# A gated-delta-rule mixer on one Trainium2 core: diagonal blocks of 43 rows instead of 32, two applications of W instead of three, and the decay matrices of a group of heads made one product earlier

## The chip, the cores and the metric

The kernel runs on one core of a Trainium2 chip. The time is the device time of one execution in microseconds (us): 2797.3 us, the median of three runs (2796.41 to 2797.56). The profile is of one execution of its own. The names of the engines are those of the profile: PE is the matrix engine (its weight loads are listed apart as PEld), DVE the vector engine, ACT the scalar engine, POOL GpSimd; SP is the queue that issues most of the DMAs.

## The reference

A two-layer decoder trunk on 256 tokens of width 2048. Each layer is a mixer, a layer norm, a gated feed-forward network, a layer norm and a gated addition. The change touches only the first layer's mixer, a gated delta rule with 16 query/key heads and 32 value heads of 128:

```python
qkv = silu(causal_dwconv(x @ w_in ..., conv_w)); q, k = l2norm(q) * 128 ** -0.5, l2norm(k)
beta = sigmoid(b); g = -exp(a_log) * softplus(a + dt_bias); gc = cumsum(g)
lmat = where(strict, (kb @ k.T) * decay, 0)          # decay = exp(gc_i - gc_j)
sol = triangular_solve(lmat + eye, [vb, kb * exp(gc)])
... o = q_dec @ S + (q k decay) @ v_new;  o * rsqrt(mean(o^2)) * norm_g * silu(z);  o @ w_o
```

The heart is a unit lower triangular system (I + L) u = rhs for each value head and each chunk of tokens.

## The kernel before, in words

**Products.** Every product with a weight matrix reads the weights in tiles of 512 KB (`weights`, L99 to L121): the SP queue fetches `raw` (four buffers), ACT makes a rounded copy `hi` (L114), DVE the rest `lo` (L115; three buffers of each), and PE multiplies with both. A tile of a transposed product (`gemm_t_steps`) is 8 matmuls of 512 columns (L147) and 8 of 256 columns (L151); one `next` or `yield` is one tile. The products of the gate z (`gemm_steps`) are L184, L187 and L190.

**Groups.** The mixer works in chunks of 128 tokens (two chunks, `a` = 0 and 1) and in eight groups g of four value heads, so a group has eight triangular systems of 128 rows (q = 8 in the shapes). The loop at the end of `gdn_groups` does for each g, in program order: `values(g)` (8 tiles of weights), `keys(g + 1)` (4 tiles for k, then 4 for q), `zgate(g + 1)` (8 tiles), `inverses(g)`, `front(g + 1)`, `mixes(g + 1)`, `substitute(g + 1)`, `solve(g)`, `outputs(g)`. For g = 0 `front`, `substitute` and `zgate` of group 0 lie inside or behind `values(0)`; for g = 7 the place of the next group's products is taken by `ahead`, twelve steps of the output product.

**One group's solution.** `front` makes L: `decays` fetches a row of sums `qd` and makes the decays on ACT (L494, L495), `sums` multiplies k with itself on PE (`g_ps<-k`, L542, L543) and makes small vectors on DVE, `blocks` makes L on DVE (L574) and sends its diagonal blocks through DRAM, so that one partition holds one block: four writes `lt` (L579) and four reads `ld` (L583), all on SP. `causal` prepares the masks for the outputs and n21, which couples the two chunks. `substitute` inverts the diagonal blocks of 32 rows on POOL, row by row: 31 steps of one multiplication (L612) and one subtraction (L614) in the tile `xi`, spread over partitions by block, head and a quarter of the columns. The result goes through DRAM: four writes `tt` (L617), four reads `pm` (L631, in `inverses`), all issued by POOL. Then `inverses` multiplies L by the block inverses (`w_ps<-pm,L`, L623) and copies what lies off the diagonal blocks to W. `solve` applies the block inverse to the right side (`s_ps<-vt,pm`) and then W three times (`s_ps<-y,W`), each followed by a subtraction on DVE (L691); with four blocks W is nilpotent of order four, and three applications are exact. It does so for chunk 0, couples by n21 (`s_ps<-u,n`), and does the same for chunk 1. In the trace, an fp32 matmul of one head has two records, so a product of four heads has eight.

**What sets the order.** The instructions are written in program order, and a planner orders each engine's instructions ahead of time by that priority and its own costs: where one isn't ready by its reckoning, a later one goes first. The splits `hi` and `lo` have a raised priority, and so has `front` of group 0. On the chip each engine runs its list in that fixed order. A tile with one buffer (L, pm, W, `ld`) can be written again only when its last reader is done.

Of the kernel before, what the change touches and what calls it, by code (L numbers as in the profile page):

```python
# [30 lines left out]
C_IDENT, C_TRI, C_QMIN, C_CMIN, C_CAUSAL, C_XINIT, C_ONES = 0, 128, 256, 384, 512, 640, 896  # L31
N_CONST = 1024


def constants():
# [6 lines left out]
    x = np.zeros((4, 32, 8, 32), np.float32)  # L42
    for cg in range(4):
        for k in range(8):
            x[cg, :, k, 4 * k + cg] = 1.0
    c[:, C_XINIT:C_XINIT + 256] = x.reshape(P, 256)
    c[:, C_ONES:C_ONES + P] = 1.0
# [16 lines left out]
class Trunk:  # L64
    def __init__(self, nc, tc, ctx, t):
# [16 lines left out]
        cst = self.cst = self.cp.tile([P, N_CONST - P], F32, tag="cst", name="cst")  # L82
        self.tri = cst[:, C_TRI - P:C_TRI - P + P]
        self.cmin = cst[:, C_CMIN - P:C_CMIN - P + P]
        self.xinit = cst[:, C_XINIT - P:C_XINIT - P + 256]
        self.ones = cst[:, C_ONES - P:C_ONES - P + P]
# [278 lines left out]
    def gdn_gates(self, pool, w, gk):  # L365
# [42 lines left out]
        nc.tensor.matmul(pc[:, 64:96], self.ones, g[:, 0], start=True, stop=True)  # L408
# [8 lines left out]
    def gdn(self, ahead):  # L417
# [3 lines left out]
        with tc.tile_pool(name="gk", bufs=1) as gk, tc.tile_pool(name="gw", bufs=1) as pool:  # L421
# [6 lines left out]
            w = pool.tile([P, 1024], F32, tag="L", name="gates")  # L428
            def load(nb, to=None):
# [3 lines left out]
                for a in range(2):  # L433
# [4 lines left out]
                         1: [(cr, t["gdn_conv_w"].rearrange("k (n c) -> n k c", c=P)), (self.cst, t["cst"][:, P:]),  # L438
# [14 lines left out]
    def gdn_groups(self, pool, gk, cw, ng, oT, load, taps, gates, ahead):  # L453
# [31 lines left out]
        def decays(s):  # L485
# [5 lines left out]
            L = s["L"] = pool.tile([P, 2, 4, P], F32, tag="L", name="L")  # L491
# [4 lines left out]

        def causal(s):

            g, dm = s["g"], s["qd"]
            do = s["qo"] = pool.tile([P, 4, P], F32, tag="qo", name="qo", bufs=2)  # L500
            for h in h4:
                nc.scalar.activation(do[:, h], dm[:, 1, h], AF.Exp, bias=self.gout[:, 4 * g + h:4 * g + h + 1])
            n21 = s["n21"] = pool.tile([P, 4, P], F32, tag="n21", name="n21", bufs=2)
            nc.vector.tensor_tensor(five(n21), bcast(s["gram"][0][:, :, P:S], 2, 2), five(do), op=ALU.mult)
# [63 lines left out]
        def blocks(s):  # L568
# [8 lines left out]
            lt = self.dr.tile([8, 4, 32, 32], F32, tag="lt", name="lt")  # L577
            for b in range(4):
                nc.sync.dma_start(out=lt[:, b].rearrange("q i j -> i q j"),  # L579
                                    in_=L[32 * b:32 * b + 32, :, :, 32 * b:32 * b + 32].rearrange("p a h j -> p (a h) j"))  # L580
            ld = s["ld"] = pool.tile([P, 32, 32], F32, tag="ld", name="ld")
            for e in h4:
                nc.sync.dma_start(out=ld[32 * e:32 * e + 32], in_=bass.AP(tensor=lt.tensor, offset=lt.offset,  # L583
                                                                          ap=[[1024, 32], [1, 1024]]))

        def mixes(s):
# [8 lines left out]
            for h in range(2):  # L595
                for a in range(2):
                    nc.tensor.matmul(pss[:, 2 * h + a:][:, 0:1], s["sq"][:, h, a * P:(a + 1) * P],
                                     self.ones[:, 0:1], start=True, stop=True)
# [4 lines left out]
        def substitute(s):  # L603


            ld = s["ld"]
            xi = pool.tile([P, 8, 32], F32, tag="xi", name="xi", bufs=2)
            tmp = pool.tile([P, 8, 32], F32, tag="xt", name="xt", bufs=2)
            nc.gpsimd.tensor_copy(xi, self.xinit.rearrange("p (c j) -> p c j", c=8))
            for i in range(31):  # L610
                w, m = 31 - i, i // 4 + 1
                nc.gpsimd.tensor_tensor(tmp[:, :m, :w], bcast(ld[:, i + 1:, i], m, 1),  # L612
                                        xi[:, :m, i:i + 1].to_broadcast([P, m, w]), op=ALU.mult)
                nc.gpsimd.tensor_tensor(xi[:, :m, i + 1:], xi[:, :m, i + 1:], tmp[:, :m, :w], op=ALU.subtract)  # L614
            tt = s["tt"] = self.dr.tile([8, 4, 8, 4, 32], F32, tag="tt", name="tt")
            for e in range(4):
                nc.gpsimd.dma_start(out=tt[:, :, :, e].rearrange("q b c j -> (q b) c j"), in_=xi[32 * e:32 * e + 32])  # L617
# [572 lines left out]
```

## Time and profile before

| what | before |
|---|---|
| median of three runs | 2797.3 us |
| the profiled execution's own time | 2797.12 us |
| its span, first to last instruction | 2795.1 us |
| PE busy | 2776.6 us (99%) |
| weight loads on PE | 2390.1 us (86%) |
| DVE busy | 1856.2 us (66%) |
| ACT busy | 1421.6 us (51%) |
| POOL busy | 337.7 us (12%) |
| DMA | 520.82 MB, mean 186 GB/s |

The span starts with the first instruction. The first mixer takes about the first 756 us of it; from group 1 to group 6 its groups repeat every 85.4 us. In a row of a timeline the first number is the start and the second the time to the end of the last of a merged row's instructions; a number behind "x" counts instructions. Matmuls overlap, so the price of a row on PE is the distance from its start to the start of the row behind it.

### The profile page before, as it was taken

How to read it: one execution, taken by the hardware profiler on the slowest of the kernel's cores; microseconds unless marked ns; L12 is line 12 of the kernel's file. 1: busy time of each engine (PE TensorE's matmuls, PEld its weight loads, DVE VectorE, ACT ScalarE, POOL GpSimd, SP SyncE). 2: the span in 40 equal slices, each digit the busy share in tenths (PEclk: the TensorE clock that was granted, in tenths of full speed). 3: DMA queues.
4: the chain of work that ended last, by engine and by line, in shares of the span. 5: the costliest groups of instructions: out<-in, count | busy, mean ns of one | idle time of the engine just before them, and what ended most of it. 6: DMA issues, size and time to landing. Idle time of an engine off the chain costs nothing. (4 is left out here: it accounts for less than half of the span.)

```text
span 2795.1 us, 40216 instructions
## 1 busy us (share of the span) xinstructions
PE 2776.6 (99%) x14958; PEld 2390.1 (86%) x14958; DVE 1856.2 (66%) x3059; ACT 1421.6 (51%) x2239; POOL 337.7 (12%) x688
## 2 busy tenths in 40 slices
PE   8999999999999999999999999999999999999999
PEld 7888888888888888888888889888888888888887
DVE  6787787877556666666545665776676666655566
ACT  4555566555445555555434544455465555543453
POOL 1543234442200000000000000120000000000000
PEclk9999999999999999999999999999999999999999
DMA  7755665655565666666556567655556666665655
GB/s 213 205 157 158 166 176 164 168 152 159 173 210 164 193 206 206 207 196 207 196 191 208 171 198 215 181 152 163 181 181 196 197 187 199 194 195 195 207 171 195
DMA packets 412275, 520.82 MB, mean 186 GB/s; under 512 B 28940, under 2 KB 301712, under 8 KB 411824
## 3 DMA queue, kind: packets, MB, share of 16 engines
q1 hardware_dynamic: 404912, 499.91, 58.9%
q0 software_dynamic: 7168, 18.35, 2.7%
q8 instruction: 117, 1.92, 0.3%
q14 instruction: 78, 0.64, 0.1%
HBM read 513.94 MB, written 7.39 MB: 187 GB/s over the span
## 5 line engine op out<-in xcount | busy, mean ns | idle before, releaser
L115 DVE TENSOR_TENSOR lo<-raw,hi 128x1024 fp32r<-128x1024 f32 (+1 forms) x921 | 1125.0, 1223 | 606.0 <-ACT hi L114 594.6
L114 ACT ACTIVATE hi<-raw 128x1024 fp32r<-128x1024 f32 (+1 forms) x921 | 967.9, 1053 | 698.9 <-PE b_ps L187 469.5
L147 PE MATMUL mm_ps<-xT,hi 128*128 128x512 f32 (+1 forms) x4176 | 1027.9, 394 | 2.6 <-ACT hi L114 2.3
L147 PEld LDWEIGHTS mm_ps<-xT,hi 128*128 128x128 f32 (+1 forms) x4176 | 762.0, 188 | 148.9 <-ACT hi L114 2.9
L151 PEld LDWEIGHTS mm_ps<-xT,lo 128*128 128x128 f32 (+1 forms) x4176 | 539.4, 191 | 22.7 <-DVE lo L115 1.5
L151 PE MATMUL mm_ps<-xT,lo 128*128 128x256 f32 (+1 forms) x4176 | 557.2, 284 | 0.4 <-DVE lo L115 0.4
L184 PE MATMUL b_ps<-hi,xT 128*128 128x512 f32 (+1 forms) x704 | 270.9, 386 | 0.0
L187 PE MATMUL b_ps<-hi,xT 128*128 128x512 f32 (+1 forms) x704 | 268.8, 383 | 0.0
L220 ACT ACTIVATE fold<-mm_ps 128x256 f32<-128x256 f32 x261 | 98.1, 376 | 268.1 <-PE mm_ps L147 267.8
L184 PE MATMUL b_ps<-hi,hTA 128*128 128x512 f32 x512 | 199.3, 389 | 0.0
L187 PE MATMUL b_ps<-hi,hTA 128*128 128x512 f32 x512 | 199.2, 389 | 0.0
L190 PE MATMUL b_ps<-lo,xT 128*128 128x512 f32 (+1 forms) x704 | 188.4, 383 | 0.0
L239 POOL DMA_DIRECT2D lng<-in_ln_g x16 | 8.8, 547 | 1239.1 <-PE b_ps L190 654.5
L612 POOL TENSOR_TENSOR xt<-ld,xi 128x60 f32<-128x60 f32 (+24 forms) x248 | 116.2, 468 | 345.1 <-DMA ld<-lt 326.3
L187 PEld LDWEIGHTS b_ps<-hi,xT 128*128 128x128 f32 x704 | 132.2, 188 | 24.8
L184 PEld LDWEIGHTS b_ps<-hi,xT 128*128 128x128 f32 x704 | 132.2, 188 | 24.1
L190 PEld LDWEIGHTS b_ps<-lo,xT 128*128 128x128 f32 x704 | 129.9, 188 | 24.5
L190 PE MATMUL b_ps<-lo,hTA 128*128 128x512 f32 x512 | 136.8, 389 | 0.0
L190 PEld LDWEIGHTS b_ps<-lo,hTA 128*128 128x128 f32 x512 | 96.1, 188 | 20.0
L184 PEld LDWEIGHTS b_ps<-hi,hTA 128*128 128x128 f32 x512 | 96.1, 188 | 20.0
L187 PEld LDWEIGHTS b_ps<-hi,hTA 128*128 128x128 f32 x512 | 96.1, 188 | 19.9
L614 POOL TENSOR_TENSOR xi<-xi,xt 128x60 f32<-128x60 f32 (+24 forms) x248 | 107.5, 433 | 19.4
(266 smaller groups left out, 2571.0 us busy)
## 6 DMA issues: line engine op xcount, KB each, us to landing
raw<-in_gdn_w_in SPq DMA_DIRECT2D x193, 512.0 KB, 4.4
raw<-in_ffn_w_gate SPq DMA_DIRECT2D x160, 512.0 KB, 4.4
raw<-in_ffn_w_up SPq DMA_DIRECT2D x160, 512.0 KB, 4.6
raw<-in_ffn_w_down SPq DMA_DIRECT2D x160, 512.0 KB, 4.1
raw<-in_dsa_w_in SPq DMA_DIRECT2D x72, 512.0 KB, 3.7
raw<-in_gdn_w_o SPq DMA_DIRECT2D x64, 512.0 KB, 4.0
raw<-in_ple_w_gate SPq DMA_DIRECT2D x64, 512.0 KB, 4.9
raw<-in_dsa_w_o SPq DMA_DIRECT2D x32, 512.0 KB, 3.9
```

The lines of the kernel that those rows point to most:

```text
L114: act = nc.scalar.activation(hi, raw, AF.Copy)
L115: ins = nc.vector.tensor_tensor(lo, raw, hi.bitcast(F32), op=ALU.subtract)
L147: ins = nc.tensor.matmul(q[:m, :], hi[:, k, o:o + m], x[:, k0 + k].rearrange("p a b -> p (a b)"), start=k0 + k == 0, stop=last)
L151: ins = nc.tensor.matmul(q[:m, S:], lo[:, k, o:o + m], x[:, k0 + k, 0, :], start=False, stop=last)
L184: ins = nc.tensor.matmul(ps[a][:, :n], xh, hi, start=k == 0, stop=False)
L187: self.before = nc.tensor.matmul(ps[a][:, :n], xl, hi, start=False, stop=False)
L190: self.last = nc.tensor.matmul(ps[a][:, :n], x(k)[:, 0, a * P:(a + 1) * P], lo, start=False, stop=k == kt - 1)
L220: nc.scalar.activation(t[:m], ps[:, S:], AF.Copy)
L239: ins = self.nc.gpsimd.dma_start(out=r, in_=bass.AP(tensor=src.tensor, offset=src.offset, ap=[[0, P], [1, n]]))
L612: nc.gpsimd.tensor_tensor(tmp[:, :m, :w], bcast(ld[:, i + 1:, i], m, 1), xi[:, :m, i:i + 1].to_broadcast([P, m, w]), op=ALU.mult)
L614: nc.gpsimd.tensor_tensor(xi[:, :m, i + 1:], xi[:, :m, i + 1:], tmp[:, :m, :w], op=ALU.subtract)
```

## The change

The diagonal blocks become 43 rows high, from rows 0, 43 and 85 (the second and the third share row 85). With three blocks W is nilpotent of order three, and W is applied twice. POOL's substitution gets 42 steps in place of 31, on 96 partitions in place of 128, with up to 132 elements a step. A block's left 22 columns and its right 21 go to DRAM and back as two tiles, `ld` and `ldr`, in six writes of 48 or 32 rows and eight reads; the inverses come back in six reads of 32 and 16 rows in place of four. The start value of `xi` is fetched from DRAM by POOL's queue for each group instead of being copied from a constant in SBUF, and the tiles `xi`, `xt` and `qo` have one buffer each in place of two. The constant of ones goes; its users take a tile set for that, or the last column of `tri`.

L gets two buffers. In the loop `front(g + 1)` moves from behind `inverses(g)` to before `zgate(g + 1)` (for g = 0, to behind `zgate(1)`, followed by seven of the eight tiles of group 1's value product). `causal` and `mixes` leave that place for `values` of their own group; n21 is made by a new function `cross` that stays in `front`, for which ACT makes the same four exponentials once more.

```diff
-C_IDENT, C_TRI, C_QMIN, C_CMIN, C_CAUSAL, C_XINIT, C_ONES = 0, 128, 256, 384, 512, 640, 896
-N_CONST = 1024
+C_IDENT, C_TRI, C_QMIN, C_CMIN, C_CAUSAL, C_XINIT = 0, 128, 256, 384, 512, 640
+B_ROWS, B_COLS, B_LEFT = 43, 11, 22
+B_FROM = (0, 43, 85)
+N_CONST = C_XINIT + B_COLS * B_ROWS
...
-            L = s["L"] = pool.tile([P, 2, 4, P], F32, tag="L", name="L")
+            L = s["L"] = pool.tile([P, 2, 4, P], F32, tag="L", name="L", bufs=2)
...
+        def cross(s):
+
+            n21 = s["n21"] = pool.tile([P, 4, P], F32, tag="n21", name="n21", bufs=2)
+            for h in h4:
+                nc.scalar.activation(n21[:, h], s["qd"][:, 1, h], AF.Exp, bias=self.gout[:, 4 * s["g"] + h:4 * s["g"] + h + 1])
+            nc.vector.tensor_tensor(five(n21), bcast(s["gram"][0][:, :, P:S], 2, 2), five(n21), op=ALU.mult)
+
         def causal(s):
 
             g, dm = s["g"], s["qd"]
-            do = s["qo"] = pool.tile([P, 4, P], F32, tag="qo", name="qo", bufs=2)
+            do = s["qo"] = pool.tile([P, 4, P], F32, tag="qo", name="qo")
...
-            n21 = s["n21"] = pool.tile([P, 4, P], F32, tag="n21", name="n21", bufs=2)
-            nc.vector.tensor_tensor(five(n21), bcast(s["gram"][0][:, :, P:S], 2, 2), five(do), op=ALU.mult)
...
-            lt = self.dr.tile([8, 4, 32, 32], F32, tag="lt", name="lt")
-            for b in range(4):
-                nc.sync.dma_start(out=lt[:, b].rearrange("q i j -> i q j"),
-                                    in_=L[32 * b:32 * b + 32, :, :, 32 * b:32 * b + 32].rearrange("p a h j -> p (a h) j"))
-            ld = s["ld"] = pool.tile([P, 32, 32], F32, tag="ld", name="ld")
-            for e in h4:
-                nc.sync.dma_start(out=ld[32 * e:32 * e + 32], in_=bass.AP(tensor=lt.tensor, offset=lt.offset,
-                                                                          ap=[[1024, 32], [1, 1024]]))
+            nl = B_ROWS - B_LEFT
+            parts = []
+            for k, n, o, tall, tag in ((B_ROWS, B_LEFT, 0, 48, "ld"), (nl, nl, B_LEFT, 32, "ldr")):
+                lead = B_FROM[-1] + o + tall - P
+                lt = self.dr.tile([8, 3, lead + tall, n], F32, tag="lt" + tag, name="lt")
+                for b, r in enumerate(B_FROM):
+                    c = r + o
+                    r0 = min(c, P - tall)
+                    at = lead - c + r0
+                    nc.sync.dma_start(out=lt[:, b, at:at + tall].rearrange("q i j -> i q j"),
+                                      in_=L[r0:r0 + tall, :, :, c:c + n].rearrange("p a h j -> p (a h) j"))
+                ld = pool.tile([96, k, n], F32, tag=tag, name="ld")
+                parts.append((lt, ld, k * n, (lead + tall) * n, lead * n))
+            for lt, ld, m, step, at in parts:
+                for e in h4:
+                    nc.sync.dma_start(out=ld[24 * e:24 * e + 24], in_=bass.AP(tensor=lt.tensor, offset=lt.offset + at,
+                                                                              ap=[[step, 24], [1, m]]))
+            s["ld"] = [x[1] for x in parts]
...
-            ld = s["ld"]
-            xi = pool.tile([P, 8, 32], F32, tag="xi", name="xi", bufs=2)
-            tmp = pool.tile([P, 8, 32], F32, tag="xt", name="xt", bufs=2)
-            nc.gpsimd.tensor_copy(xi, self.xinit.rearrange("p (c j) -> p c j", c=8))
-            for i in range(31):
-                w, m = 31 - i, i // 4 + 1
-                nc.gpsimd.tensor_tensor(tmp[:, :m, :w], bcast(ld[:, i + 1:, i], m, 1),
-                                        xi[:, :m, i:i + 1].to_broadcast([P, m, w]), op=ALU.mult)
-                nc.gpsimd.tensor_tensor(xi[:, :m, i + 1:], xi[:, :m, i + 1:], tmp[:, :m, :w], op=ALU.subtract)
+            ld, right = s["ld"]
+            xi = pool.tile([96, B_COLS, B_ROWS], F32, tag="xi", name="xi")
+            nc.gpsimd.dma_start(out=xi, in_=t["cst"][:96, C_XINIT:])
+            for i in range(B_ROWS - 1):
+                w, m = B_ROWS - 1 - i, i // 4 + 1
+                col = ld[:, i + 1:, i] if i < B_LEFT else right[:, i + 1 - B_LEFT:, i - B_LEFT]
+                tmp = pool.tile([96, 132], F32, tag="xt", name="xt")[:, :m * w].rearrange("p (c j) -> p c j", c=m)
+                nc.gpsimd.tensor_tensor(tmp, bcast(col, m, 1), xi[:, :m, i:i + 1].to_broadcast([96, m, w]), op=ALU.mult)
+                nc.gpsimd.tensor_tensor(xi[:, :m, i + 1:], xi[:, :m, i + 1:], tmp, op=ALU.subtract)
...
-            for b in range(4):
-                nc.gpsimd.dma_start(out=pm[32 * b:32 * b + 32, :, 32 * b:32 * b + 32],
-                                    in_=s["tt"][:, b].rearrange("q c e j -> (c e) q j"))
+            for b, r in enumerate(B_FROM):
+                o = int(b > 1)
+                for k, n in ((o, 32), (B_ROWS - 16, 16)):
+                    nc.gpsimd.dma_start(out=pm[r + k:r + k + n, :, r + o:r + B_ROWS],
+                                        in_=s["tt"][:, b].rearrange("q c e j -> (c e) q j")[k:k + n, :, o:])
...
-                mul(s["L"][:, a], pm[:, 4 * a:4 * a + 4, 32:], ps)
+                mul(s["L"][:, a], pm[:, 4 * a:4 * a + 4, B_ROWS:], ps)
...
+            else:
+                causal(s)
+                if g > 1:
+                    for _ in range(3):
+                        next(steps)
+                mixes(s)
             self.go_(steps)
...
-                for i in range(3):
+                for i in range(2):
                     ps = mul(W[:, a], y)
...
-            causal(s)
+            cross(s)
...
                 n = keys(g + 1, rest)
+                if g:
+                    front(n)
                 zgate(n, [])
+                if not g:
+                    front(n)
+                    for _, _ in zip(range(7), begin(n)[0]):
+                        pass
...
             inverses(s)
             if g < 7:
-                front(n)
-                mixes(n)
                 substitute(n)
             solve(s)
```

`begin` makes the steps of a group's value product once and hands them to `values` again.

More of the change, by code (lines that the diff above doesn't have):

```diff
@@ L41, in constants @@
     c[:, C_CMIN:C_CMIN + P] = np.where(j <= i, np.float32(3.4e38), np.float32(-BIG))
[L42 to L47, printed above, removed]
+    x = np.zeros((4, 24, B_COLS, B_ROWS), np.float32)
+    for n in range(B_ROWS):
+        x[n % 4, :, n // 4, n] = 1.0
+    c[:96, C_XINIT:] = x.reshape(96, B_COLS * B_ROWS)
     c[:, C_CAUSAL:C_CAUSAL + P] = j <= i
@@ L407, in gdn_gates @@
         nc.tensor.matmul(pc[:, 0:64], self.tri, g64, start=True, stop=True)
-        nc.tensor.matmul(pc[:, 64:96], self.ones, g[:, 0], start=True, stop=True)
+        ones = pool.tile([P, P], F32, tag="y0", name="ones")
+        nc.gpsimd.memset(ones, 1.0)
+        nc.tensor.matmul(pc[:, 64:96], ones, g[:, 0], start=True, stop=True)
         nc.tensor.matmul(pc[:64, 128:256], g64, self.tri, start=True, stop=True)
@@ L427, in gdn @@
             cr = pool.tile([64, 4, P], F32, tag="ld", name="cr")
-            w = pool.tile([P, 1024], F32, tag="L", name="gates")
+            w = pool.tile([P, 1024], F32, tag="L", name="gates", bufs=2)
             def load(nb, to=None):
@@ L628, in inverses, with begin @@
         def inverses(s):
-            for b in range(4):
-                nc.gpsimd.dma_start(out=pm[32 * b:32 * b + 32, :, 32 * b:32 * b + 32],
-                                    in_=s["tt"][:, b].rearrange("q c e j -> (c e) q j"))
-            for a in range(2):
-                ps = self.sp.tile([P, 4, 96], F32, tag="bk", name="w_ps")
-                mul(s["L"][:, a], pm[:, 4 * a:4 * a + 4, 32:], ps)
-                for b in (1, 2, 3):
-                    nc.scalar.activation(W[:32 * b, a, :, 32 * b:32 * b + 32], ps[:32 * b, :, 32 * b - 32:32 * b], AF.Copy)
+            for b, r in enumerate(B_FROM):
[3 more added lines that the diff above has]
+                                        in_=s["tt"][:, b].rearrange("q c e j -> (c e) q j")[k:k + n, :, o:])
+            for a in range(2):
+                ps = self.sp.tile([P, 4, P - B_ROWS], F32, tag="bk", name="w_ps")
+                mul(s["L"][:, a], pm[:, 4 * a:4 * a + 4, B_ROWS:], ps)
+                for r, n in ((B_ROWS, B_ROWS), (2 * B_ROWS, P - 2 * B_ROWS)):
+                    nc.scalar.activation(W[:r, a, :, r:r + n], ps[:r, :, r - B_ROWS:r - B_ROWS + n], AF.Copy)
+        def begin(s):
+            g = s["g"]
+            v = pool.tile([P, 4, S], F32, tag="v", name="v")
+            if "v" in s:
+                return s["v"]
+            s["v"] = self.gemm_t_steps(w_in, 4096 + 512 * g, 512, self.xT, conv(32 + 4 * g, lambda n: v[:, n])), v
+            return s["v"]
         def values(s):
             g = s["g"]
-            v = pool.tile([P, 4, S], F32, tag="v", name="v")
-            steps = self.gemm_t_steps(w_in, 4096 + 512 * g, 512, self.xT, conv(32 + 4 * g, lambda n: v[:, n]))
+            steps, v = begin(s)
             if not g:
```

15 lines of the change are left out of this document (7 added, 8 removed).

## The prediction, made before the changed kernel was run

> **What bounds the kernel now.** I read the page first, its busy times and slices.
>
> ```profile
> span 2795.1 us, 40216 instructions
> PE 2776.6 (99%) x14958; PEld 2390.1 (86%) x14958; DVE 1856.2 (66%) x3059; ACT 1421.6 (51%) x2239; POOL 337.7 (12%) x688
> POOL 1543234442200000000000000120000000000000
> PEclk9999999999999999999999999999999999999999
> ```
>
> PE has work for 99% of the span at the full granted clock, and POOL's substitution fills only the first eleven slices. Second, the waits of PE up to 1000 us:
>
> ```profile
> PE t_ps L231 <- DMA x_in<-in_x: 5.1, 1, 5.1
> PE mm_ps L147 <- ACT hi L114: 2.3, 2, 1.8
> ```
>
> The first is the start of the kernel. In the groups PE waits for nothing worth naming: neither for the weights, nor for POOL's chain, nor for DVE between two applications of W, since the planner puts weight matmuls between them. So a matmul taken away is time taken away, as long as no new wait appears. Third, PE's timeline, for the price of what goes and the place of what moves:
>
> ```profile
> 138.80 1.92 PE L623 MATMUL w_ps<-pm,L 128*128 128x96 f32 x16
> ...
> 202.27 0.48 PE L184 MATMUL b_ps<-hi,xT 128*128 128x512 f32 x1
> ...
> 204.20 1.07 PE L190 MATMUL b_ps<-lo,xT 128*128 128x512 f32 x4
> ...
> 206.92 1.07 PE L190 MATMUL b_ps<-lo,xT 128*128 128x512 f32 x4
> ...
> 224.16 1.92 PE L623 MATMUL w_ps<-pm,L 128*128 128x96 f32 x16
> 225.91 0.62 PE L542 MATMUL g_ps<-k 128*128 128x256 f32 x2
> ...
> 227.25 1.06 PE L623 MATMUL s_ps<-vt,pm 128*128 128x128 f32 x8
> 228.06 2.10 PE L147 MATMUL mm_ps<-xT,hi 128*128 128x512 f32 x8
> 230.00 2.07 PE L151 MATMUL mm_ps<-xT,lo 128*128 128x256 f32 x16
> 231.91 3.82 PE L147 MATMUL mm_ps<-xT,hi 128*128 128x512 f32 x16
> 235.56 2.08 PE L151 MATMUL mm_ps<-xT,lo 128*128 128x256 f32 x16
> ...
> 243.52 1.05 PE L623 MATMUL s_ps<-y,W 128*128 128x128 f32 x8
> 244.33 1.19 PE L151 MATMUL mm_ps<-xT,lo 128*128 128x256 f32 x8
> 245.36 1.15 PE L623 MATMUL s_ps<-y,W 128*128 128x128 f32 x8
> 246.27 1.20 PE L151 MATMUL mm_ps<-xT,lo 128*128 128x256 f32 x8
> ```
>
> The product for W (`w_ps`) comes every 224.16 - 138.80 = 85.4 us. Before the second one stand the z products, from 202.27 on (21.9 us); behind it stand the products k with k (1.34 us, to 227.25), which begin the next group's L. A tile of z costs 206.92 - 204.20 = 2.72 us, a tile of v (231.91 to 235.56 and on, 3.65 us for 16 `hi`; 230.00 to 231.91, 1.91 us for 16 `lo`; half of both) 2.78 us.
>
> **What the change takes off PE.** One application of W goes in each of 8 groups and 2 chunks: 16 times eight records. One costs 244.33 - 243.52 = 0.81 us or 246.27 - 245.36 = 0.91 us; the mean of the two, 0.86, gives 13.8 us. Interleaving has a price as well: eight `lo` between two applications take 245.36 - 244.33 = 1.03 us, against 1.91 / 2 = 0.955 in the dense row; 16 x 0.08 = 1.2 us go too. Together **-15.0 us** (ends: 16 x 0.81 = -13.0 and 16 x 0.99 = -15.8).
>
> The product for W shrinks from 96 to 85 columns, but its 16 records of 96 columns cost 225.91 - 224.16 = 1.75 us (0.109 each), while eight of 128 columns cost 228.06 - 227.25 = 0.81 us (0.101 each): here the width doesn't set the price. By width it would be 8 x 1.75 x 11 / 96 = -1.6 us; I take 0 and keep -1.6 and, as the start inside a tile may cost too, +1.6. The products of `front` and `mixes` only move. DVE loses 16 subtractions and ACT gains 32 exponentials:
>
> ```profile
> L691 DVE TENSOR_TENSOR y<-y,s_ps 128x512 f32<-128x512 f32 x32 | 22.0, 686 | 24.5 <-PE s_ps L623 24.4
> L502 ACT ACTIVATE qo<-qd,go 128x128 f32<-128x128 f32 x32 | 11.5, 390 | 8.4 <-DMA qd<-grow 8.4
> ```
>
> That is 16 x 0.686 = -11.0 us of DVE, and on ACT 32 x 0.390 = +12.5 us (and 16 copies to W fewer), spread over eight groups. Both engines stand under the splits' needs (51% and 66%) and PE doesn't wait for them, so I count 0; if that cover were gone, one split late per group would cost at most its 1.2 us, 10 us in all.
>
> **What gets longer: POOL's substitution.** Its timeline, and the DVE and window rows that explain it:
>
> ```profile
> 89.23 0.78 POOL L612 TENSOR_TENSOR xt<-ld,xi 128x31 f32<-128x31 f32 x1 [25.91 <-DMA ld<-lt]
> ...
> 90.48 0.25 POOL L612 TENSOR_TENSOR xt<-ld,xi 128x30 f32<-128x30 f32 x1
> ...
> 103.15 0.35 POOL L614 TENSOR_TENSOR xi<-xi,xt 128x76 f32<-128x76 f32 x1
> ...
> 131.87 2.33 POOL L631 DMA_DIRECT2D pm<-tt  x4 [3.71 <-DMA tt<-xi]
> ...
> 250.20 0.38 POOL L612 TENSOR_TENSOR xt<-ld,xi 128x31 f32<-128x31 f32 x1 [44.94 <-DMA ld<-lt]
> ...
> 252.54 1.21 POOL L612 TENSOR_TENSOR xt<-ld,xi 128x28 f32<-128x28 f32 x1
> ```
> ```profile
> 252.42 1.23 DVE L115 TENSOR_TENSOR lo<-raw,hi 128x1024 fp32r<-128x1024 f32 x1
> ```
> ```profile
> 250.20:282.70 32.50, 27.68 (x62) 1.00 0.49 136
> 89.20:125.50 36.30, 31.49 (x62) 1.00 0.63 183
> ```
> From a later stretch of POOL's timeline, and from the view of the tile pm:
>
> ```profile
> 287.19 2.33 POOL L631 DMA_DIRECT2D pm<-tt  x4 [1.91 <-PE mm_ps L147]
> ```
> ```profile
> DMA to landing us min/median/max: 3.2/4.7/6.6
> ```
>
> In the window rows stand the stretch, POOL's busy time and the count. Thirty elements take 0.25 us and 76 take 0.35, that is 2.2 ns an element; between two instructions lie (32.50 - 27.68) / 62 = 0.08 us. Some take 1.2 us: the one at 252.54 lies on DVE's split at 252.42 and ends with it. The 31 steps before have 1560 elements a partition (the sum of (31 - i)(i // 4 + 1)), 50 a step; the 42 steps after have 3663, 87 a step. So 62 x (0.29 + 0.08) = 23 us undisturbed become 84 x (0.37 + 0.08) = 38 us. The rest, 32.5 - 23 = 9.5 us, is mostly splits in the way and grows with the time that is exposed to them: 9.5 x 38 / 23 = 16. I take **52 us** (group 0, among the denser splits of z: 38 + 13.3 x 38 / 23 = 60, or by the count of instructions 38 + 13.3 x 84 / 62 = 56; I take 58). Bounds: 84 x 0.45 = 38 with no split in the way, and, if the price were all in the elements, 27.68 x 3663 / 1560 + 84 x 0.08 = 72.
>
> [...]
>
> **Where L comes earlier.** k with k now begins 1.34 + 21.9 = 23.2 us before `w_ps` instead of 1.75 us behind its start. From there to POOL's first step took 250.20 - 225.91 = 24.3 us. Two more writes lie ahead of the left reads:
>
> ```profile
> 214.96 23.52 SPq L109 DMA_DIRECT2D raw<-in_gdn_w_in  x8
> 238.53 2.02 SPq L579 DMA_DIRECT2D lt<-L  x4
> 243.65 0.39 SPq L109 DMA_DIRECT2D raw<-in_gdn_w_in  x1
> 244.28 1.70 SPq L583 DMA_DIRECT2D ld<-lt  x4
> ```
>
> At 0.5 us each that makes 25.3: POOL starts 2.1 us behind `w_ps` instead of 26. It ends at 2.1 + 52 = 54; to the first `pm` issue it took 287.19 - 282.70 = 4.5 us (6.4 in group 0, from 125.50 to 131.87); six issues at 0.58 are 3.5 us, the landing 4.7. So pm is there at 67 to 69 us, and the next `w_ps` is due at 85.4 less two removed applications, 83.5. **Slack of some 15 us** from group 2 on; before it was 224.16 + 85.4 - (287.19 + 2.33 + 4.7) = 15.3. The fetch of `xi`, which with one buffer waits for the `tt` writes of the group before, has only the substitution's steps behind it on POOL and lies in the idle time ahead of them (44.94 us in the row above, some 20 after). The last group gains 24 us of lead and pays 52 - 32.5 + 1.2 = 21. So 0 here.
>
> The first two groups are tight. Group 0: POOL starts at 89.2 + 1 and ends at 148; `pm` is issued at 154.6 and lands at 162.8. PE reaches `w_ps` at 138.80 + 1.34 + 7 x 2.78 = 159.6: 3 us late. Group 1: k with k at 138.80, POOL starts at 164.1, ends at 216, pm lands at 230; PE comes 85.4 - 19.5 - 1.8 = 64 us after group 0's `w_ps`, at 227: 3 us late. Nominally 6; with the shorter end of each term 0, with the longer 12. The planner may fill a part: I take **+4 us**. Later groups do not inherit it.
>
> **The sum.** The profiled execution took 2797.12 us around its span of 2795.1: 2797.12 - 15.0 + 4 = 2786.1. The median of the runs is 0.2 above it, so 2786.3; I say **2786**.
>
> **The rivals.** (A) *The weights' queue is held.* SP stands between the first `lt` and the last `ld` from 238.53 to 245.98 (244.28 + 1.70), 7.5 us, with one weight tile between. After, it is 6 x 0.5 + 3.1 (the wait for the landing, 240.55 to 243.65) + 8 x 0.43 = 9.6 us, moved from the solving, where PE has other work, into the z products, which eat a tile every 2.72 us and in which SP issues eight in 23.52 us. What is in the buffers, four raw and two splits, covers 6 x 2.72 = 16.3 us, less a landing and the two splits:
>
> ```profile
> raw<-in_gdn_w_in SPq DMA_DIRECT2D x193, 512.0 KB, 4.4
> L114 ACT ACTIVATE hi<-raw 128x1024 fp32r<-128x1024 f32 x905 | 955.9, 1058 | 684.4 <-PE b_ps L187 459.9 <-PE mm_ps L147 133.5 <-ACT hi L114 17.9
> ```
>
> 16.3 - 4.4 - 1.06 - 1.23 = 9.6 us. It decides as soon as SP also waits for L: 3.5 us a group would be 8 x 3.5 = 28, and 2786 + 28 = 2814, slower. For it: the two numbers are equal. Against it: the planner puts tiles between, as at 243.65. Chance 0.10.
>
> (B) *POOL is late in every group*, which needs a substitution over 52 + 15 = 67 us, near its upper bound of 72. The price at 72, with group 0 at 31.49 x 3663 / 1560 + 7 = 81: group 0 is 3 + 23 = 26 us late; POOL is free for group 1 only at 181, whose pm then lands at 181 + 72 + 12.7 = 266 against PE's 186 + 64, 16 us late; from group 2 on 2.1 + 72 + 12.7 = 87 stands against 83.5, 3.3 us in each of at least five. That is 58 in place of the 4: 2840. Against it: 30 and 76 elements differ by 0.1 us only. Chance 0.04.
>
> (C) *The gain is given back at the start and in the solving*: 12 us late in groups 0 and 1 (the longer ends), or splits late by 10 us: 2782 + 12 = 2794, no change. Nothing in the rows excludes it; for the first half speak the tight sums above. Chance 0.14.
>
> (D) *The forecast*, 2779 to 2791: chance 0.72; its lower end is -15.8 - 1.6 with no lateness.
>
> **How the numbers follow.** What a measurement of this kernel can tell from no change I put at 0.2%, 5.6 us: faster is below 2791.7, slower above 2802.9. D is faster; of C a fifth is faster and the rest splits into no change (0.10) and slower (0.01); A splits evenly between no change and slower, with a little slower more; B is slower. Faster 0.75, same 0.14, slower 0.11. The range runs from 2779 to 2798, which leaves the far halves of A and B out.
>
> **What would show it.** The records of `s_ps<-y,W` fall from 384 to 256, and the distance between two `w_ps` from 85.4 to about 83.5 us from group 2 on. POOL's substitution takes 48 to 56 us from group 1 on and starts within 4 us of `w_ps`. PE waits before `w_ps` in groups 0 and 1, by 6 us at most. It is wrong if PE waits for `hi` in the z products (A), for pm in later groups (B), or if the distance falls and the total doesn't (a stage behind the mixer has changed).

## The result: slower, and the profile after

The changed kernel takes 2819.57 us (median of 4 runs, 2818.57 to 2821.65) against 2796.86 us of the kernel before on the same chip: a ratio of 1.0082, with a 95% interval of 1.0070 to 1.0094. That is 22.7 us slower, where 2786 us, 11 faster, had been forecast. The profiled execution took 2818.95 us around its span of 2817.2 us.

The head of the page and the waits of PE up to 1000 us, of the kernel after (waits: the waiting instruction, what it waited for, us in total, times, longest):

```profile
span 2817.2 us, 40266 instructions
PE 2770.7 (98%) x14830; PEld 2380.9 (85%) x14830; DVE 1873.6 (67%) x3043; ACT 1428.5 (51%) x2255; POOL 488.7 (17%) x881
...
PE w_ps L638 <- DMA pm<-tt: 16.3, 2, 12.1
...
PE ss_ps L612 <- DVE qd L606: 4.3, 6, 0.8
PE g_ps L547 <- ACT vt L690: 3.6, 5, 1.0
...
PE g_ps L548 <- ACT vt L690: 1.5, 6, 0.3
```

PE has fewer instructions (14830 against 14958: the 16 times eight of the removed applications) and a little less busy time, but it now waits inside the groups, which it didn't do before. There are two kinds of waits. Two are long: for pm, in the first and the last group. Many are short, each under 1.1 us: ahead of the gram (`g_ps`) and of the sums of squares (`ss_ps`), in nearly every group.

The long waits cost more than their length. PE's timeline at the two W products, and windows there (us, busy us and count of PE, PEld, DVE, ACT, POOL, then the granted clock, the DMA share and GB/s), of the kernel after:

```profile
171.31 3.71 PE L638 MATMUL w_ps<-pm,L 128*128 128x85 f32 x16 [12.07 <-DMA pm<-tt]
...
747.17 3.68 PE L638 MATMUL w_ps<-pm,L 128*128 128x85 f32 x16 [4.22 <-DMA pm<-tt]
```
```profile
159.00:171.50 12.50, 0.43 (x4) 0.23 (x3) 1.70 (x3) 0.45 (x1) 3.91 (x7) 0.66 0.88 217
171.50:180.00 8.50, 8.50 (x49) 8.28 (x50) 1.38 (x2) 1.60 (x5) 5.35 (x18) 0.70 0.11 26
...
163.00:176.70 13.70, 5.39 (x25) 5.39 (x26) 0.00 (x0) 1.01 (x4) 4.79 (x14) 0.50 0.62 173
180.00:200.00 20.00, 18.88 (x128) 16.49 (x127) 16.33 (x33) 11.93 (x36) 17.49 (x33) 1.00 0.28 80
...
747.00:760.00 13.00, 12.83 (x66) 11.53 (x67) 3.42 (x7) 2.66 (x6) 0.00 (x0) 0.75 0.06 22
```

PE stops at 159.2 (171.31 - 12.07). About 3.8 us later, at 163.0, the granted clock falls to one half, and it stays there for some 5.4 us after work has begun again, to 176.7: 13.7 us at half clock. The 16 records of the W product take 3.71 us there; 16 records of 96 columns took 1.92 us before. The same happens around the 4.22 us wait that ends at 747.17: the clock falls at 746.7, again 3.8 us into the wait, and comes back at 753.5, after 6.8 us at 0.50.

POOL's timeline behind the substitution of group 0, of the kernel after:

```profile
147.66 1.08 POOL L629 TENSOR_TENSOR xi<-xi,xt 96x11 f32<-96x11 f32 x1
149.04 2.79 POOL L632 DMA_DIRECT2D tt<-xi  x4 [0.29 <-POOL xi L629]
160.52 1.79 POOL L648 DMA_DIRECT2D pm<-tt  x3 [8.69 <-issue]
164.11 1.19 POOL L648 DMA_DIRECT2D pm<-tt  x2 [1.80 <-DMA pm<-tt]
165.78 0.53 POOL L648 DMA_DIRECT2D pm<-tt  x1 [0.47 <-DMA pm<-tt]
```

The substitution ends at 148.7, near the forecast 148, but that is in part luck: POOL began 2.2 us late (92.4 against 90.2) and was 1.7 us quicker than forecast (56.3 against 58). And pm lands only with the W product's start, 22.6 us later, where the prediction had 14.8. The third row shows 8.7 us between the issue of `tt` and the first fetch of pm. The fourth and fifth show something that isn't in the kernel before: a fetch of pm waits for another fetch of pm. In the change's loop over `(o, 32), (B_ROWS - 16, 16)` the rows 27 to 31 of a block (27 to 32 in the third) are written twice, so the second fetch is held until the first has landed.

Where the time went is best read from the starts of the W products, with the kernel `two_steps` (below), which differs from the one after only in that POOL's substitution is nearly empty, as the measure of what the change could have brought (differences of starts in us, rounded to 0.1):

| us | before | two_steps | after |
|---|---|---|---|
| start of the span to W product 0 | 138.8 | 159.9 | 171.3 |
| 0 to 1 | 85.4 | 64.4 | 70.0 |
| 1 to 6 (five groups) | 426.7 | 416.7 | 428.3 |
| 6 to 7 | 75.6 | 70.6 | 77.6 |
| 7 to the end of the span | 2068.6 | 2067.2 | 2070.0 |
| span | 2795.1 | 2778.8 | 2817.2 |

The first two lines belong together, since the order of work moves 21 us of PE's work ahead of W product 0. Without the substitution the change is worth 16.3 us. The substitution costs 38.4 us: 17 by W product 1, 11.6 in the five groups in the middle, 7.0 in the last group and 2.8 behind it.

### The profile page after: what moved, and what is told of

The parts are those of the page before. It is cut to its first block, busy times and chain, and to the rows that moved or that the text cites. A ratio compares the mean times of both kernels' runs of the same rounds, so it can differ in the third digit from the quotient of the medians.

```text
span 2817.2 us, 40266 instructions
## 1 busy us (share of the span) xinstructions
PE 2770.7 (98%) x14830; PEld 2380.9 (85%) x14830; DVE 1873.6 (67%) x3043; ACT 1428.5 (51%) x2255; POOL 488.7 (17%) x881
## 5 line engine op out<-in xcount | busy, mean ns | idle before, releaser
L628 POOL TENSOR_TENSOR xt<-ld,xi 96x120 f32<-96x120 f32 (+5 forms) x336 | 179.5, 534 | 164.9 <-DMA ld<-lt 132.7
L629 POOL TENSOR_TENSOR xi<-xi,xt 96x120 f32<-96x120 f32 (+5 forms) x336 | 185.1, 551 | 26.3
```

Of the source, the lines that this page charges most:

```text
L628: nc.gpsimd.tensor_tensor(tmp, bcast(col, m, 1), xi[:, :m, i:i + 1].to_broadcast([96, m, w]), op=ALU.mult)
```

## The experiments

**The two halves of the change, each alone.** `two_in_old` is the kernel before with one application of W less; it leaves out the third of three, which its 32-row blocks need:

```diff
-                for i in range(3):
+                for i in range(2):
```

> The kernel before with W applied twice instead of three times and nothing else changed (it leaves out the third application, which blocks of 32 rows need). Theory 1, the applications were PE time and PE time alone, as the prediction had it: 16 x 0.86 us and their interleaving go, the total falls by 15 us to about 2782, the distance between two products for W from 85.4 to 83.5 us. Rival, the chain of a group's solution (matmul, subtraction, matmul) sets the pace and the weight matmuls only fill it: below 4 us, 2793 to 2797.

Measured: 2777.59 us, ratio 0.9929 (0.9912 to 0.9946), 19.5 us less than the 2797.12 us of the kernel before on that chip. The removed PE work is worth its full time.

`order_alone` is the kernel before with the new order, L held twice and qo, xi and xt once; blocks of 32 rows and three applications stay.

```diff
+                if g:
+                    front(n)
                 zgate(n, [])
...
-                front(n)
-                mixes(n)
                 substitute(n)
```

> The kernel before (blocks of 32 rows, three applications) in the changed order: L twice, front before the z products, causal and mixes in values, seven tiles of group 1's v ahead; for space qo, xi and xt have one buffer. Theory 1, the new order itself costs PE three short waits a group (two at k with k, one at the sums of q), 2.2 us by the changed kernel's groups: 87.5 us from one product for W to the next, about 2811. Rival, the loss comes from the higher blocks alone (late pm, late transfers): 85.4 us and 2797.

Measured: 2797.62 us, ratio 1.000 (0.999 to 1.001). A miss: the order costs nothing. Its row for the W product shows that the first one stands at 159.6 there too, against 138.8 before, because of the work put ahead of it:

```profile
L628 PE MATMUL w_ps<-pm,L x128: 243/275/275, 159.6 to 729.3; 128*128 128x96 f32 x128
```

`blocks_alone` is the other half: 43-row blocks and two applications in the order of before.

> The 43-row blocks and the two applications of W in the order of before (gram, L, q products and substitution of the next group behind the W product of this one; L held once). Theory: POOL can start 31 us behind the W product (26 to 28 us before, and 5 us more for the longer chain of fetches), substitutes 52 us and needs 20 us until pm has landed: 103 us, against a group of 83 us of TensorE work, so groups 1 to 7 wait some 18 us each: 2795 - 19 + 7 x 18 = 2902 us (2870 to 2930). Rival (the order isn't needed, POOL is hidden): 2795 to 2805 us.

Measured: 2917.45 us, ratio 1.0432 (1.0411 to 1.0453), inside the expected range. The waits are shorter than expected, 14 us on average for 18, but PE waits for pm in all eight groups and not in seven, and the granted clock falls in each (0.978 over the span):

```profile
PE w_ps L633 <- DMA pm<-tt: 112.8, 8, 19.6
```

So the longer substitution needs the new order, and the order by itself, with blocks of 32 rows, is free. The 22.7 us come from the blocks inside that order.

**Is it POOL's work?** `two_steps` is the kernel after with 2 of the 42 steps of the substitution; what it computes is no longer the mixer.

```diff
-            for i in range(B_ROWS - 1):
+            for i in range(2):
```

> The kernel after with 2 of the 42 steps of the substitution on POOL; the other 40 are left out, so what it computes isn't the mixer any more. The order of all that is left, the DMAs and the two applications of W stay. Theory 1 (the long substitution on POOL slows VectorE by contention, and this makes the small waits of TensorE ahead of the gram and of ss_ps): the mean of the convolution's steps on VectorE falls from 541 ns to about 484, the waits of TensorE ahead of g_ps and ss_ps all but vanish, and the distance between two W products falls from 85.45 to 83.2 us; with the late pm gone too, 2778 to 2784 us. Rival (the small waits come from the order and the PSUM slots alone): they stay, the distance stays above 85 us, and only the 24 us of the late pm in groups 0 and 7 are gained: 2793 to 2798 us.

Measured: 2781.23 us, ratio 0.9945 (0.9930 to 0.9960). The first theory holds: PE's waits for pm, at `ss_ps` and behind `vt` are gone, and W products come every 83.3 us (416.7 / 5) in place of 85.7 (428.3 / 5). VectorE tells why. Its rows between W products 1 and 6, first after, then with two steps (busy us, mean ns):

```profile
L479 DVE SCALAR_TENSOR_TENSOR ac<-pd,cw,ac 128x256 f32<-128x256 f32 x120 | 62.0, 542 | 0.0
L513 DVE SCALAR_TENSOR_TENSOR qd<-qd,gc,cst 128x128 f32<-128x128 f32 x40 | 19.0, 486 | 0.2
...
L747 DVE SCALAR_TENSOR_TENSOR ot<-o_ps,rs,zs 128x128 f32<-128x128 f32 x40 | 11.2, 337 | 0.0
L482 DVE SCALAR_TENSOR_TENSOR v<-v,ac 128x256 f32<-128x256 f32 x20 | 10.8, 561 | 0.0
...
L714 DVE SCALAR_TENSOR_TENSOR vt<-s_ps,nc,vt 128x128 f32<-128x128 f32 x20 | 5.6, 345 | 0.4
```
```profile
L479 DVE SCALAR_TENSOR_TENSOR ac<-pd,cw,ac 128x256 f32<-128x256 f32 x120 | 54.2, 479 | 0.0
L513 DVE SCALAR_TENSOR_TENSOR qd<-qd,gc,cst 128x128 f32<-128x128 f32 x40 | 13.4, 347 | 0.6
...
L747 DVE SCALAR_TENSOR_TENSOR ot<-o_ps,rs,zs 128x128 f32<-128x128 f32 x40 | 11.2, 343 | 0.0
L482 DVE SCALAR_TENSOR_TENSOR v<-v,ac 128x256 f32<-128x256 f32 x20 | 8.0, 419 | 0.0
...
L714 DVE SCALAR_TENSOR_TENSOR vt<-s_ps,nc,vt 128x128 f32<-128x128 f32 x20 | 5.6, 345 | 0.6
```

With the full substitution on POOL, the convolution's steps take 542 ns on average in place of 479, the masking of qd 486 in place of 347, the last step of v 561 in place of 419. Two rows of the same operation that read one of their inputs from PSUM also fall into the substitution (in one group they run at 422 and at 445 to 448 us, and POOL substitutes from 419.4 to 471.4), and they don't get longer: 337 against 343 ns (`ot`) and 345 in both (`vt`). The three rows that got longer, by 13, 40 and 34%, read two tensors in SBUF. So do the splits `lo`, which got 2% longer (1252 ns against 1222). Why the one kind is slowed and the other isn't, these rows don't show.

**Why a slower VectorE stops PE.** PE's timeline of the kernel after at the gram:

```profile
387.93 0.60 PE L688 MATMUL v_ps<-ident,v 128*128 128x128 f32 x4
389.12 1.13 PE L547 MATMUL g_ps<-k 128*128 128x256 f32 x4 [0.60 <-ACT vt L690]
```

The gram takes a PSUM slot that transposes of v have filled (the first ones start at 384.69), and must wait until ScalarE has emptied it. ScalarE is late because VectorE is, as two rows of ScalarE's timeline show:

```profile
384.83 0.42 ACT L481 ACTIVATE k<-ac 128x256 f32<-128x256 f32 x1 [1.31 <-DVE ac L479]
...
387.96 1.12 ACT L690 ACTIVATE vt<-v_ps,sv 128x128 f32<-128x128 f32 x4
```

The step that waits for the convolution starts 0.1 us behind those transposes; in a later group of `two_steps` it starts 2.3 us ahead of them (611.65 against 613.95), and `vt` is done before the gram. `ss_ps` stands in the same way behind the reads of the q product. In `psum_apart` the gram takes the other pair of slots, and `ss_ps` spare columns of the q product's second tile:

```diff
-            s["gram"] = gram(s["k"], s["k"])
+            s["gram"] = gram(s["k"], s["k"], "bk")
...
-            pss = self.sp.tile([P, 4], F32, tag="sp", name="ss_ps")
+            pss = self.spare
```

> The changed kernel with front's k with k in the other pair of PSUM slots and the sums of q in the spare columns of the mixes' second tile. Theory 1, PE's three short waits a group are for a free PSUM slot (held by v's transposition and by the mixes): they go, 85.5 us from one product for W to the next become 83.5, and the total falls by 12 to 14 us to about 2806. Rival, PE waits there for data of DVE and ACT (k, q, the squares), and the place doesn't matter: within 3 us of 2819.6.

Measured: 2812.18 us, ratio 1.0053 (1.0038 to 1.0068), 7.4 us less than after, where 12 to 14 had been expected. The waits behind `vt` are gone; `ss_ps` still waits, now for reads of the tile that it shares:

```profile
PE g_ps L614 <- DVE qd L608: 6.5, 8, 1.1
```

**The late pm.** `pm_apart` reads pm in pieces that don't overlap:

```diff
-                for k, n in ((o, 32), (B_ROWS - 16, 16)):
+                for k, n in ((o, 32), (o + 32, B_ROWS - 32 - o)):
```

> The changed kernel with the inverses fetched by 32 and 11 rows (10 in the third block) that don't overlap, instead of 32 and 16 that share five rows. Theory 1, the second read of a block waits for the landing of the first because both write the shared rows: without it the six reads are issued in 3.5 us instead of 5.8, pm lands 3 to 4 us earlier, PE's wait before group 0's product for W falls from 12.1 to some 8.5 us, that of the last group (4.2 us, with the half clock behind it) goes, and the total falls by 7 to 11 us to about 2810. Rival, the landing of the tt writes is what is late, or 11 rows go slower than 16: no earlier landing, 2817 to 2823.

Measured: 2805.42 us, ratio 1.0032 (1.0019 to 1.0045), 14 us less than after. Its six fetches of pm leave without a stop, and W product 0 starts 4.7 us earlier:

```profile
159.46 3.47 POOL L648 DMA_DIRECT2D pm<-tt  x6 [7.72 <-issue]
...
166.64 3.71 PE L638 MATMUL w_ps<-pm,L 128*128 128x85 f32 x16 [7.40 <-DMA pm<-tt]
```

From the end of the substitution to pm it takes 17.9 us in group 0 and 12.7 to 16.4 in the others (after: 22.5 and 17.2 to 20.0; before: 12.4 and 10.7 to 13.1). The gain is more than group 0's 4.7 us: the last group's wait also falls, to 2.2 us, and no slow stretch follows it. (The profiled execution shows 10.4 us of the 14 in its span, 2806.8 us: it was the slowest of the five runs.)

`front_early` is the kernel after with the front part of group 1 ahead of the z products in group 0 too, so that the small packets of its L are written before the substitution of group 0 ends; its `ld` goes through POOL's queue.

```diff
-                if g:
-                    front(n)
+                front(n)
                 zgate(n, [])
                 if not g:
-                    front(n)
```

> The kernel after with one thing moved: in group 0 the front part of group 1 (its gram, L and the writes of L to DRAM) ahead of the z products of group 1, as in the later groups, so that its many small packets no longer lie between the substitution of group 0 and pm; its ld is fetched through POOL's queue behind pm. Theory (these packets are what makes the tail of group 0 22.6 us long, where 14.6 were forecast): the tail falls by 4 to 8 us, to 15 to 18 us, and the first W product starts at 164 to 167 us in place of 171.3. Rival (the tail is long because of the overlapping pm reads and the 172-byte pieces alone, as in the later groups, where it is 20 us): 20 us or more, W product at 169 us or later. For the whole kernel, since the ld of group 1 now waits for pm of group 0 and the substitution of group 1 sets the next W product, 2814 to 2820 us either way.

Measured: 2814.56 us (2 runs), ratio 1.0065 (1.0044 to 1.0085). The tail of group 0 is 19.3 us in place of 22.5, W product 0 starts at 167.1: between the two expectations. The neighbour's packets are 3 us of the tail in this kernel, and 4.4 us where the reads of pm don't overlap (`best5` against `best2`, below), each from one execution.

**The half clock.** `filled` is the kernel after with 46 matmuls that compute nothing ahead of W product 0 and 17 ahead of W product 7.

> The kernel after, with 46 matmuls of 512 columns that compute nothing put ahead of the W product of group 0 and 17 ahead of that of group 7, so that TensorE isn't idle while pm is on its way. Theory 1 (the idle time lowers the granted clock, and the work behind it is run at half speed): the granted clock stays at 1.0 through both places, and the kernel gains what the slow stretches cost, 2.7 us behind group 0 and 3.1 us behind group 7: 2814 us (2812 to 2816). Rival (the slow stretches cost nothing, something else holds the work there): 2819 to 2821. Second rival (the added matmuls push real work back): 2822 or more.

Measured: 2811.69 us, ratio 1.0053 (1.0037 to 1.0070), 7.9 us less than after. Same windows as above, now at the full clock:

```profile
159.00:171.50 12.50, 12.50 (x67) 10.68 (x66) 1.50 (x2) 0.95 (x4) 3.21 (x9) 1.00 0.81 221
171.50:180.00 8.50, 8.50 (x61) 7.65 (x60) 3.58 (x8) 1.81 (x5) 6.93 (x21) 1.00 0.01 1
```

W product 0 starts 1.85 us earlier there (pm landed earlier, at 167.8), W product 1 gains another 2.12, and W products 6, 7 and the end 0.85, 0.21 and 2.07 more: 7.1 in this execution. The 2.12 and the 2.07 stand right behind the stretches that were slow, so by this estimate the half clock cost some 4 us; the rest isn't separated from where pm lands. The 2.12 is net: this execution has a slow stretch of its own, of 3.4 us from 194.7 on, which the one of the kernel after hasn't.

**Repairs together.** `best1` has pm in disjoint pieces, `tt` laid out so that each partition writes one contiguous piece, and both the gram and `ss_ps` in the other pair of PSUM slots.

> The kernel after with three repairs: pm is read in pieces that don't overlap; the gram of the front part and ss_ps take the other pair of PSUM slots; tt is laid out so that each partition writes 1892 contiguous bytes, and pm reads rows out of it. Theory (three separate losses, which add): 14 us as with pm alone, 10 us for the PSUM slots (7.4 measured with the wait at ss_ps left), 4 us for a shorter tail from tt to pm: 2791 us (2787 to 2796), faster than both. Rival (the repairs overlap, the lateness of group 0 is set by the substitution): 2797 to 2802 us, no faster than before.

Measured: 2827.59 us, ratio 1.0109 (1.0094 to 1.0124): slower than all. The slot that `ss_ps` gets there is held by the outputs of the group before:

```profile
PE ss_ps L615 <- DVE ot L760: 24.2, 7, 4.0
```

There are seven waits of 2.0 to 4.0 us, and each is followed by a stretch of 3.4 or 6.8 us at half clock (0.992 over the span): W products come every 90 us. A wait for PSUM was exchanged for a longer one. `best2` computes `ss_ps` right behind the q product into spare columns of its tile, ahead of VectorE's reads, and takes all eight value steps of group 1 ahead of W product 0:

```diff
             p1, p2 = gram(k, q)
+            pss = self.spare
+            ... the four products of ss_ps, moved up
...
-                    for _, _ in zip(range(7), begin(n)[0]):
+                    for _, _ in zip(range(8), begin(n)[0]):
```

> The kernel after with the three repairs again, but ss_ps computed right behind the q product into spare columns of its second PSUM tile, ahead of VectorE's reads of it, so that it waits neither for those reads nor for the outputs of the group before; and all 8 value steps of group 1 ahead of the W product of group 0 in place of 7. Theory (the repairs are good, the kernel with all three lost its gain to the 24 us of waits at ss_ps alone and to the half clock behind them): no wait at ss_ps, 12.9 us from the end of the substitution to pm, a W product of group 0 near 162 us with a wait under 2 us, a distance of 83.5 to 84.2 us between W products, and 2785 to 2791 us, faster than before. Rival (the new layout of tt or the 8 steps cost something of their own): 2797 us or more.

Measured: 2793.22 us (11 runs), ratio 0.9983 (0.9974 to 0.9992): a little faster than before, 2 us short of what was expected. From W product 2 to 6 the distance is 83.3 us, that of `two_steps`, although VectorE is as slow as in the kernel after (536 ns for the convolution's steps):

```profile
L482 DVE SCALAR_TENSOR_TENSOR ac<-pd,cw,ac 128x256 f32<-128x256 f32 x120 | 61.3, 536 | 0.4
```
```profile
PE w_ps L643 <- DMA pm<-tt: 7.3, 2, 5.8
...
PE ot_ps L768 <- DVE ot L762: 2.7, 2, 2.4
```

So the short waits need both: the slower VectorE and the shared PSUM slots. What is left are the waits in groups 0 and 1 and the last. `best3` is `best2` with the layout of `tt` of the kernel after:

> As the other kernel of this call, but with the layout of tt of after; of the DMA side only pm is read in pieces that don't overlap. Theory (the tail from the substitution to pm is longer by 4 to 5 us than with the new layout, which the last group and group 0 alone can feel): 3 to 8 us slower than the other one, 2790 to 2796 us. Rival (the tail of these groups is hidden by the eighth value step): equal to the other within 2 us.

Measured: 2796.23 us, ratio 0.9996 (0.9987 to 1.0004): by the medians of eleven runs each the layout is worth 3 us, the lower end of the expectation; the single runs overlap (2789.9 to 2795.5 and 2792.9 to 2801.3). `best4` is `best2` with 26 and 8 empty matmuls ahead of W products 0 and 7:

> The kernel with the new layout of tt and all 8 value steps ahead (2793 us), with 26 matmuls that compute nothing ahead of the W product of group 0 and 8 ahead of that of group 7. Theory (the half clock behind the 5.8 us wait of group 0 costs 2 to 3 us; the wait itself stays, since pm sets it): granted clock 1.0 behind it, 2789 to 2791 us. Rival (a wait that short does not lower the clock, or the filler delays real work): 2793 us or more.

Measured: 2793.09 us, ratio 0.9987 (0.9978 to 0.9996). The profiled execution had its W product 1 at 229.7 in place of 233.2 and no wait for pm, but the medians are equal and the runs spread over 5 us (2790.2 to 2795.1): inconclusive for a wait as short as 5.8 us. `best5` is `best2` with the move of `front_early`:

> The kernel of 2793 us (all three repairs, 8 value steps ahead) with the same move. Theory (packets of group 1 lengthen the tail of group 0): from the end of the substitution to pm 13 to 14 us in place of 18.4, the first W product at 161 to 163 us; the second W product is then set by POOL's chain of group 1 at 231 to 234 us as now, so the total stays within 2 us of 2793. Rival (the move lets group 1 start earlier too): 2788 us or less. Second rival (the ld through POOL's queue makes group 1 later): 2796 us or more.

Measured: 2798.33 us, ratio 1.0006 (0.9997 to 1.0016): no faster than before, as the second rival had it. W product 0 comes in time, and the next is late instead:

```profile
162.02 1.21 PE L643 MATMUL w_ps<-pm,L 128*128 128x85 f32 x9 [0.33 <-DMA pm<-tt]
...
236.08 1.34 PE L643 MATMUL w_ps<-pm,L 128*128 128x85 f32 x5 [8.55 <-DMA pm<-tt]
```

POOL begins group 1's substitution at 168.8 in both kernels; in `best5` it waits there for `ld`, which comes through POOL's queue behind pm. It ends it 2.4 us later (219.7 against 217.3), and pm takes 1.6 us longer from there; why isn't separated. That time won for group 0 must be lost in group 1 isn't shown: in `pm_apart` W product 1 kept the 4.7 us that W product 0 had won.

## Why the prediction was wrong, step by step

The forecast was -15 us for what goes and +4 us for lateness. By the spans in the table the first came out as -16.3 and the second as +38.4. So the step that failed is the cost of POOL's longer substitution: 4 us for a late pm in groups 0 and 1, and 0 everywhere else. The places are these.

**What goes off PE: right in kind, too small.** The 16 applications leave, and their time with them: -19.5 us in `two_in_old` against -15.0. In one group of its trace, the applications' own records give 1.73 us (forecast 16 x 0.86 / 8 = 1.72), but the weight products and solving products around them take another 0.55 us less, where the prediction had 1.2 / 8 = 0.15 for interleaving. That term was read from one stretch of eight `lo`.

**"The products of `front` and `mixes` only move", and "DVE and ACT: I count 0": the step that failed in every group.** The priced cover was that PE doesn't wait for these engines. POOL's longer substitution made VectorE slower, and the products that moved stand right behind other users of their PSUM slots. Together this is 2.3 us a group ((428.3 - 416.7) / 5), in which the 2 us per group that the missing applications bring in the middle (426.7 - 416.7 = 10.0) are lost entirely. The prediction counted what VectorE's splits add to POOL's steps (16 of its 52 us) and nothing the other way; the rows above show the other way too, 542 ns in place of 479 for the convolution's steps. It named "one split late per group, 10 us in all" as the price of the lost cover, which is near the 11.6 us, but as an upper end and in rival C.

**The substitution: right.** 56.3 us in group 0 (58 forecast), 47.9 in group 1 and 51.8 to 52.4 from group 2 on (52). Its start in group 1 was not: POOL waits 6.5 us there for the fetch of `xi`, which the prediction had placed in idle time, and begins at 173.3 instead of 164.1. PE doesn't wait for that, since its W product 1 comes only at 241.3.

**"POOL starts 2.1 us behind `w_ps`": 5 us short.** In the last group the gram starts at 645.85 and POOL's first step at 676.26:

```profile
645.85 1.13 PE L547 MATMUL g_ps<-k 128*128 128x256 f32 x4 [0.91 <-ACT vt L690]
```
```profile
676.26 0.27 POOL L628 TENSOR_TENSOR xt<-ld,xi 96x42 f32<-96x42 f32 x1 [18.73 <-DMA ld<-lt]
```

That is 30.4 us against the 25.3 forecast. In `two_steps` it is 29.6 (617.62 to 647.23), so it doesn't come from POOL; the prediction had carried over the distance from another place in the group, with two writes added. From group 2 to 6 the slack of 15 us took this up.

**The tail from the substitution to pm: the mis-sized term of groups 0 and 7.** Forecast 14.8 and 12.7 us, from the kernel before; measured 22.5 and 18.4. The runs show two additions in group 0: 4.7 us for the overlapping fetches, which stand in the diff and were not read, and 3 to 4.4 us for the neighbour's packets, which the change moves into that time. With both taken away and the new layout of `tt` (`best5`) the tail is 14.0. The step "+4 us lateness" became a wait of 12.1 us.

**"The last group: so 0 here": failed.** Gram to POOL 5 us over, tail 5.7 over: of the 3 us that were left of its lead nothing remained, and the 4.2 us wait brought the half clock.

**The half clock wasn't in any rival.** The slice row of before showed the full clock throughout, and the prediction priced a wait at its length alone.

**The rivals.** C, the gain given back at the start and in the solving, is what happened, but it was priced as one or the other (2794); both came, with the clock on top. A didn't happen: PE never waits for `hi` in the z products. B didn't either: from group 2 to 6 pm is in time. (In A's sum the three terms make 9.5 us, not 9.6, which changes nothing.)

Of the signs named: the records of `s_ps<-y,W` are 256, and the substitution is as long as was said. The start within 4 us of `w_ps`, the distance of 83.5 us, the waits in groups 0 and 1 (they are in groups 0 and 7) and their limit of 6 us are wrong, and each points at one of the steps above.

## What to carry to other kernels

- The longer chain on an idle engine wasn't free for its neighbours here: three rows of VectorE with two inputs in SBUF took 542 ns in place of 479, 486 in place of 347 and 561 in place of 419, and two with one input in PSUM took no longer. Look which instructions run beside such a chain, price them by a run of the same form elsewhere in the trace, and ask which PSUM slot is emptied later by it.
- Where one transfer's target overlapped another's in this kernel, the second was made to wait for the first to land (4.7 us in group 0); cut pieces so that they are disjoint, even if one gets smaller.
- A wait of PE of some 4 us (4.22, in the last group) cost its length and, at half clock, some 2 us behind it (2.07, by the difference to `filled`). Shortening one stage of a chain that two groups share on one engine can move the wait to the next group, as in `best5`.

## What the runs showed of the hardware that had not been expected

- In the kernel after, the granted clock fell from 1.00 to 0.50 about 3.8 us after PE went idle, at both long waits, and came back 5.4 and 6.4 us after work had begun again. The slow stretches inside the first mixer last 3.4 us or a multiple of it (13.7 and 6.8 in the kernel after, up to 20.5 in `blocks_alone`), and one, in `best1`, came without PE idle for a whole 3.4 us before it. Windows at two short waits, of `best1` (2.04 us) and of `pm_apart` (2.21 us), each of 3.4 us and the 3.4 us behind them:

```profile
715.30:718.70 3.40, 1.36 (x10) 1.19 (x10) 3.40 (x10) 0.60 (x1) 3.09 (x5) 1.00 0.73 230
718.70:722.10 3.40, 3.40 (x14) 3.08 (x14) 0.99 (x4) 1.06 (x1) 2.93 (x7) 0.50 0.47 154
```
```profile
736.65:740.06 3.41, 1.50 (x7) 0.93 (x5) 1.46 (x2) 1.06 (x1) 0.00 (x0) 1.00 0.78 252
740.06:743.48 3.42, 3.11 (x26) 3.10 (x27) 0.00 (x0) 1.16 (x5) 0.00 (x0) 1.00 0.47 166
```

  With PE busy for 1.36 of 3.40 us the next 3.40 ran at half clock; with 1.50 of 3.41 the next didn't, and in `filled` the clock fell behind 3.40 us with PE busy for 2.38. So neither the length of a wait nor this busy time tells alone in these runs whether the clock falls; what does stays open.
- The same small DMAs took longer in company: the four writes of `tt` (44.3 KB each) took a median 2.4 us to land in `blocks_alone`, where PE, VectorE, ScalarE and the weight fetches all stood still, and 5.3 us in the kernel after. The rows of the DMA view and of the windows for these stretches (147 to 158 us, and 149 to 171 us), of `blocks_alone` and of the kernel after; the last two figures of a window row are the DMA share and GB/s:

```profile
tt<-xi POOLq DMA_DIRECT2D x4, 44.3 KB, 2.4
...
146.70:158.00 11.30, 0.00 (x0) 0.00 (x0) 0.00 (x0) 0.00 (x0) 6.71 (x12) 0.50 0.26 41
```
```profile
tt<-xi POOLq DMA_DIRECT2D x4, 44.3 KB, 5.3
...
148.70:171.30 22.60, 10.55 (x60) 9.05 (x58) 11.78 (x22) 6.31 (x10) 6.75 (x12) 0.82 0.85 184
```

  In `blocks_alone` the whole tail is 11.2 us, with the overlapping fetches still in it. How much of the rest is queueing behind the weights and how much the 172-byte pieces of `tt` wasn't separated. Nor does company alone settle it: in the kernel before, the four writes of 32 KB took a median 3.7 us in group 0 and 2.2 us in group 2, both beside weight fetches.
